# Gate/up products of chunk pairs by seven block products, behind a scaled norm, in a two-layer hybrid network on one core

## The chip, the core and the metric

The kernel runs on one core of a Trainium2 chip. The metric is the device time of one execution in microseconds (us). The engines named below are TensorE (PE, matrix products and transposes, with PEld for its weight loads), VectorE (DVE), ScalarE (ACT), GpSimd (POOL) and SyncE (SP, which issues nearly all DMAs).

## What is computed

The input is one sequence of 256 rows with 1024 features, all in f32. Two layers follow each other. Each has a feed-forward, a mixer and a second feed-forward, each added to the residual stream `h` behind an RMS norm.

```python
def rmsnorm(x, w):
    xf = x.astype(jnp.float32)
    y = xf * lax.rsqrt(jnp.mean(xf * xf, axis=-1, keepdims=True) + EPS)
    return (y * w.astype(jnp.float32)).astype(x.dtype)

def swiglu(x, w_gu, w_down):
    g, u = jnp.split(x @ w_gu, 2, axis=-1)
    return (jax.nn.silu(g) * u) @ w_down
...
    for layer in range(DEPTH):
        h = h + 0.5 * swiglu(rmsnorm(h, ffn1_norm[layer]), ffn1_wgu[layer], ffn1_wd[layer])
        hn = rmsnorm(h, mix_norm[layer])
        ...
        h = h + 0.5 * swiglu(rmsnorm(h, ffn2_norm[layer]), ffn2_wgu[layer], ffn2_wd[layer])
    return rmsnorm(h, final_norm)
```

`w_gu` is 1024 x 5632 (2816 gate columns, then 2816 up columns) and `w_down` 2816 x 1024. The mixer of the first layer is retention and gated linear attention, that of the second a gated linear recurrence and an mLSTM. Both have an input projection of 3600 or 2568 columns, a chain of small work, and an output projection of 1024 x 1024. The change does not touch their arithmetic.

## The kernel before

**Rows and products.** The 256 rows are two halves of 128 (t = 0 and 1). The f32 product is made of three one-pass products: `split` (L101 to L104) writes the high part of a tensor on ACT and the rest, the low part, on DVE, and `mm3` (L181 to L189) adds high x high (L185), high x low weights (L186) and low x high weights (L188). The transposed rows are the stationary operand (128 x 128), the weights the moving one (512 columns at a time).

**Weights.** `load_group` (L109 to L140) brings a group of 128 x 2048 (1 MB) into a `raw` buffer (3 of them) by DMAs of SP and splits it in pieces of 1024 columns (L103, L104; 512 beside the mixers) into `hi` and `lo` buffers (5 of each).

**A feed-forward** (`ffn_units`) has eleven chunks of 256 hidden columns. `a_unit(j)` loads chunk j's 256 gate and 256 up columns, and multiplies each half of the rows: 8 blocks of 128 features x 3 products of 512 columns into one PSUM tile. ACT then makes the silu of the gate (L359), DVE the product with the up half (L361), and PE transposes the result a little later (L201), whose split is `aT`. `b_unit(j)` multiplies `aT` with the chunk's rows of `w_down` into two accumulators `acc` of 512 columns. The units run in the order a0, a1, b0, a2, b1 and so on. The last b unit adds half of `acc` to `h` (`update`) and calls `norm`.

**The norm** (L266 to L288) transposes `h` as it stands (L279), and weights each of the eight blocks as it splits it (`split_w`, L215 and L217). The scale of a row, 1/rms, is computed beside it (`sumsq`) and applied later, where the products are read from PSUM: `scale=rs` on L359, `scalar=rs` on L361, and in the mixers' evacuations. The final norm (L315 to L336) is different: its scale is known before its last multiplication.

**Order.** The second half of the rows follows 1.5 units (LAG) behind the first. Small work is put between the products: `defer(n, fn)` runs `fn` after n more chunks of products or when its result is needed (`flush`). Each engine runs its queue in order, and a tile scheduler writes that order. Constants of a mixer are loaded 14 units ahead of it (`early`).

Of the kernel before, what the change touches and what calls it, by code (L numbers as in the profile page):

```python
# [29 lines left out]
LAG = 1.5  # L30
# delays, in 512-column chunks of the products
# [21 lines left out]
def hybrid_kernel(ctx: ExitStack, tc: tile.TileContext, I, out):  # L53
# [5 lines left out]
    apool = ctx.enter_context(tc.tile_pool(name="act", bufs=1))  # L59
    psum = ctx.enter_context(tc.tile_pool(name="psum", bufs=4, space=bass.MemoryType.PSUM))  # L60
# [40 lines left out]
    def split(src2, hi2, lo2):  # L101
        """src = hi + lo exactly, both carried by one-pass products"""
        S.activation(hi2, src2, AF.Copy)  # L103
        V.tensor_tensor(out=lo2, in0=src2, in1=hi2.bitcast(F32), op=ALU.subtract)  # L104
# [4 lines left out]
    def load_group(src, a, b, fine=False, step=1024, hook=None):  # L109
        """one streamed weight group, seen as [128, a, b] with a * b <= 2048; hook is told of each part to be split"""  # L110
# [70 lines left out]
    def mm3(outs, xT, k, wk, start, stop):  # L181
        """outs: list of (psum, column slice) sharing the stationary chunk k; wk: (hi, lo) views [128, cols]"""
# [13 lines left out]
    def transpose_into(src, n, xT, k0, w=None):  # L196
        """n (<= 4) chunks of 128 columns of src -> xT[:, k0 : k0 + n] in split form, times w by channel"""
# [39 lines left out]
    def norm0(w):  # L237
        """the first norm, among the splits of the first weights"""
# [27 lines left out]
    def norm(t, w, wait=None):  # L266
        """transposed, split, weighted residual; the row scale is left to the evacuations"""
# [3 lines left out]
        def tr():  # L271
            # neighbouring chunks lie in different banks, which the engines then read at one time
# [16 lines left out]

    def get_x(t):  # L290
        flush(lambda: state["xT"][t] is not None)
        return state["xT"][t]
# [5 lines left out]
    # the table set of the feed-forward is there before its first use  # L298
# [7 lines left out]
    def open_pool(name):  # L306
        mixstack.close()
        pools.append(mixstack.enter_context(tc.tile_pool(name=name, bufs=1)))

# [5 lines left out]
    def final_part(t, n):  # L315
        """half of the row: its share of the mean square, and the product with the weights; then the scale"""
# [22 lines left out]
    def ffn_units(wgu, wd, nxt, layer0=False):  # L339
# [4 lines left out]
        def a_unit(j):  # L344
# [4 lines left out]
            def run(t, w):  # L349
                xT = get_x(t)  # L350
                if j == 0:
                    st["acc"][t] = [ps_tile(tag="acc") for _ in range(2)]
                ps = ps_tile()
                for k in range(KC):
# [4 lines left out]
                state["act"] = S.activation(s, ps[:, :FCH], AF.Silu, scale=rs)  # L359
                a = apool.tile([P, FCH], F32, tag="ffa", bufs=2, name=nm("ffa"))  # L360
                state["dve"] = V.scalar_tensor_tensor(out=a, in0=ps[:, FCH:], scalar=rs, in1=s, op0=ALU.mult,  # L361
                                                      op1=ALU.mult)
                aT = [apool.tile([P, 2, P], F32R, tag=f"aT{x}", bufs=4, name=nm("aT")) for x in "hl"]
# [7 lines left out]
        def b_unit(j):  # L371
# [3 lines left out]
            def run(t, w):  # L375
                flush(lambda: (t, j) in st["aT"])
                aT = st["aT"].pop((t, j))
                acc = st["acc"][t]
# [10 lines left out]
                if j == NCHUNK - 1 and nxt is None:  # L389
                    # one half is done while the other is still in the products  # L390
# [8 lines left out]
                if j == NCHUNK - 1:  # L399
                    for n in range(2):  # L400
                        update(n)
                    norm(t, NW[nxt])
            return load, run

        units.append(a_unit(0))
# [769 lines left out]
```

## Time and profile before

| what | before |
|---|---|
| median of 3 runs | 1005.92 us (1005.69 to 1006.1) |
| span of the profiled execution, first to last instruction | 1004.4 us |
| instructions | 12334 |
| DVE: 1024-column and smaller splits of weights and results (L104) | 400, 398.8 us |
| ACT: the same splits' high parts (L103) | 400, 342.7 us |
| PE: products of the three kinds into `ps` | 3 x 928, 357 to 364 us each |
| HBM read, written | 176.15 MB, 1.05 MB |

```profile
DVE  6654545576576654545465455545878765555453
ACT  7544444484455644444454445444998764444442
...
DMA  8956564645247565565656565655334656656521
...
q1 hardware_dynamic: 129736, 177.22, 55.1%
```

These are the page's busy digits: the span is cut in 40 slices, and each digit is the busy share of an engine in tenths. The feed-forwards lie where DVE stands at 4 to 6, the mixers where it rises to 7 and 8. The last line is the queue with nearly all transfers: packets, megabytes, and its share of the sixteen DMA engines' time.

### The profile page before, as it was taken

To read this page: it belongs to the slowest core of one execution; us is meant where nothing else is said; L and a number is where in the kernel's file an instruction comes from. 1 tells how busy PE (TensorE), PEld (TensorE's weight loads), DVE (VectorE), ACT (ScalarE), POOL (GpSimd) and SP (SyncE) were. 2 spreads that over 40 slices of the span, in tenths; PEclk is the share of its full clock that TensorE was granted. 3 is DMA by queue.
4 is the path that set the end of the run, shared out by engine and by line. 5 is a ranking of instruction groups with operands and counts; after the bars stand their busy time and mean duration, and the time that the engine had idled before them with its cause. 6 is when DMAs were issued, how large, how long until landed. Compare 5 with 4: busy or idle time off the path is not lost.

```text
span 1004.4 us, 12334 instructions
## 1 busy us (share of the span) xinstructions
PE 989.5 (99%) x4704; PEld 813.0 (81%) x4704; DVE 585.9 (58%) x945; ACT 529.0 (53%) x877; POOL 22.5 (2%) x54
## 2 busy tenths in 40 slices
PE   7999999999999999999999999999999999999997
PEld 5888888887888888888888888888988888888885
DVE  6654545576576654545465455545878765555453
ACT  7544444484455644444454445444998764444442
POOL 1000000000100000000000000000000000000000
PEclk9999999999999999999999999999999999999999
DMA  8956564645247565565656565655334656656521
GB/s 276 311 177 200 172 206 149 190 132 172 95 168 227 163 210 192 176 202 170 207 168 205 163 205 161 206 167 153 127 126 139 218 168 209 207 166 205 165 96 42
DMA packets 129796, 178.01 MB, mean 177 GB/s; under 512 B 8756, under 2 KB 104900, under 8 KB 129736
## 3 DMA queue, kind: packets, MB, share of 16 engines
q1 hardware_dynamic: 129736, 177.22, 55.1%
q8 instruction: 37, 0.61, 0.2%
q14 instruction: 23, 0.19, 0.1%
HBM read 176.15 MB, written 1.05 MB: 176 GB/s over the span
## 4 chain that ended last, share of the span: by engine, by line
PE 92%; ACT 3%; DMA 2%; DVE 1%; issue 1%; SPq 0%; POOLq 0%; POOL 0%; ACTq 0%
PE ps L185 19%; PE ps L188 19%; PE ps L186 19%; PE acc L185 9%; PE acc L188 9%; PE acc L186 9%; PE ps L201 2%; DMA raw<-in_ffn_wgu_dram 2%; ACT hi L103 1%; DVE lo L104 1%; DMA cum<-in_c_cum_dram 0%; PE acc L615 0%; PE acc L618 0%; PE acc L279 0%; PE acc L481 0%
## 5 line engine op out<-in xcount | busy, mean ns | idle before, releaser
L104 DVE TENSOR_TENSOR lo<-raw,hi 128x1024 fp32r<-128x1024 f32 (+3 forms) x400 | 398.8, 1029 | 262.4 <-ACT hi L103 260.8
L103 ACT ACTIVATE hi<-raw 128x1024 fp32r<-128x1024 f32 (+3 forms) x400 | 342.7, 900 | 244.5 <-PE ps L188 138.1
L185 PE MATMUL ps<-hi,Th 128*128 128x512 f32 (+3 forms) x928 | 364.2, 392 | 1.3 <-ACT Th L215 1.3
L188 PE MATMUL ps<-hi,Tl 128*128 128x512 f32 (+3 forms) x928 | 357.3, 385 | 0.0
L186 PE MATMUL ps<-lo,Th 128*128 128x512 f32 (+3 forms) x928 | 356.6, 384 | 0.0
L185 PEld LDWEIGHTS ps<-hi,Th 128*128 128x128 f32 x928 | 175.3, 189 | 34.7 <-ACT Th L215 1.7
L188 PEld LDWEIGHTS ps<-hi,Tl 128*128 128x128 f32 x928 | 175.0, 189 | 34.6 <-issue 0.2
L186 PEld LDWEIGHTS ps<-lo,Th 128*128 128x128 f32 x928 | 175.5, 189 | 31.8 <-DVE lo L104 0.2
L185 PE MATMUL acc<-hi,aT 128*128 128x512 f32 x352 | 142.7, 405 | 0.0
L186 PE MATMUL acc<-lo,aT 128*128 128x512 f32 x352 | 138.9, 394 | 0.0
L359 ACT ACTIVATE ffs<-ps,rs 128x256 f32<-128x256 f32 x88 | 41.8, 474 | 154.0 <-PE ps L188 154.0
L188 PE MATMUL acc<-hi,aT 128*128 128x512 f32 x352 | 111.0, 395 | 0.0
L361 DVE SCALAR_TENSOR_TENSOR ffa<-ps,rs,ffs 128x256 f32<-128x256 f32 x88 | 42.4, 481 | 92.4 <-ACT ffs L359 92.4
L188 PEld LDWEIGHTS acc<-hi,aT 128*128 128x128 f32 x352 | 66.1, 188 | 15.1
L186 PEld LDWEIGHTS acc<-lo,aT 128*128 128x128 f32 x352 | 66.5, 189 | 13.8
L185 PEld LDWEIGHTS acc<-hi,aT 128*128 128x128 f32 x352 | 66.5, 189 | 13.4
L104 DVE TENSOR_TENSOR aT<-ps,aT 128x256 fp32r<-128x256 f32 x88 | 36.8, 418 | 7.5 <-ACT aT L103 7.5
L103 ACT ACTIVATE aT<-ps 128x256 fp32r<-128x256 f32 x88 | 32.8, 373 | 11.6 <-PE ps L201 11.6
L201 PEld LDWEIGHTS ps<-ident,ffa 128*128 128x128 f32 x176 | 24.6, 140 | 12.3 <-DVE ffa L361 0.6
L201 PE MATMUL ps<-ident,ffa 128*128 128x128 f32 x176 | 33.6, 273 | 0.1
L215 ACT ACTIVATE Th<-ps,nw 128x128 fp32r<-128x128 f32 x56 | 21.0, 375 | 12.9 <-PE ps L279 11.3
L185 PE MATMUL acc<-hi,Th 128*128 128x512 f32 x64 | 25.3, 399 | 0.0
(269 smaller groups left out, 535.9 us busy)
## 6 DMA issues: line engine op xcount, KB each, us to landing
raw<-in_ffn_wgu_dram SPq DMA_DIRECT2D x168, 512.0 KB, 4.9
raw<-in_ffn_wd_dram SPq DMA_DIRECT2D x44, 1024.0 KB, 4.9
raw<-in_e_w_in_dram SPq DMA_DIRECT2D x13, 1024.0 KB, 5.0
raw<-in_o_w_in_dram SPq DMA_DIRECT2D x9, 1024.0 KB, 5.1
raw<-in_e_w_out_dram SPq DMA_DIRECT2D x4, 1024.0 KB, 5.0
raw<-in_o_w_out_dram SPq DMA_DIRECT2D x4, 1024.0 KB, 5.0
raw<-in_ffn_wgu_dram SPq DMA_DIRECT2D x14, 256.0 KB, 6.3
rope<-in_c_rope_dram SPq DMA_DIRECT2D x4, 256.0 KB, 3.9
```

Source lines behind the costliest of these rows:

```text
L103: S.activation(hi2, src2, AF.Copy)
L104: V.tensor_tensor(out=lo2, in0=src2, in1=hi2.bitcast(F32), op=ALU.subtract)
L185: T.matmul(ps, xh[:, k, :], wk[0][:, sl], start=start, stop=False)
L186: T.matmul(ps, xh[:, k, :], wk[1][:, sl], start=False, stop=False)
L188: state["mm"] = T.matmul(ps, xl[:, k, :], wk[0][:, sl], start=False, stop=stop)
L201: T.transpose(pt[:, i * P:(i + 1) * P], src[:, i * P:(i + 1) * P], ident)
L215: last = S.activation(hi, p_, AF.Copy, scale=w[:, k:k + 1])
L359: state["act"] = S.activation(s, ps[:, :FCH], AF.Silu, scale=rs)
L361: state["dve"] = V.scalar_tensor_tensor(out=a, in0=ps[:, FCH:], scalar=rs, in1=s, op0=ALU.mult, op1=ALU.mult)
```

## The change

**Which chunks.** Of the eleven chunks of a feed-forward, six are now made in three pairs; the others are single as before. In the first feed-forward of the network the chunks run 0, 1, then pair 2+3, 4, pair 5+6, 7, pair 8+9, 10; in the other three 0 (its units placed ahead of the rest), pair 1+2, 3, pair 4+5, 6, pair 7+8, 9, 10.

**A pair.** Two chunks together have 512 gate columns G and 512 up columns U. Features are cut in two halves (blocks 0 to 3 and 4 to 7), rows in two halves as well, so that the weights are four 1 MB blocks: r11 (first features, G), r12 (first, U), r21 (second, G), r22 (second, U). The plain way makes eight block products, each of 4 feature blocks x 3 products of 512 columns. The pair makes seven (P1 to P7, Strassen's scheme in Winograd's form): 84 products in place of 96. For that it needs sums of weight blocks, made in place on DVE with 2048 columns an instruction (r12 + r11 for P5; r22 - r12 for P6; r12 - r11 for P7; r21 + r12 for P4), sums of the rows' blocks (S1 to S4, once for each feed-forward), and sums of the results (`cs` tiles). The wide blocks are loaded into `draw` buffers (4), split into the same `hi` and `lo` rings, 2048 columns an instruction, and each result is transposed in four blocks.

**The norm.** Sums over both halves of the rows need rows that are already scaled. `norm_f` therefore computes the row scale first (two sums of squares on ACT, L328 on DVE, the power on POOL), then scales `h` by it and by the norm weights, which a DMA of 512 KB spreads over all partitions (`load_wB`), and transposes the result `hs`. Evacuations of such a feed-forward use no scale. The first feed-forward keeps the old norm for chunks 0 and 1 and gets `norm_f` in addition.

**Order.** A feed-forward is no longer a row of units that the two halves pass 1.5 units apart: its middle part is written out (`main`), with down-projection units (`fill`) between the block products. Down units and output-projection units count half a unit for LAG. The mixer's constants are opened at the feed-forward's last chunk instead of 14 units ahead. There are 8 `aT` buffers instead of 4.

```diff
+PLAN = {
+    True: dict(head=(0, 1), mid=("D2", "a4", "D5", "a7", "D8"), tail=(10,)),
+    False: dict(head=(0,), mid=("D1", "a3", "D4", "a6", "D7", "a9"), tail=(10,)),
+}
+
+TAILB = 3
...
+    def norm_f(t, scaled=False, wait=NT):
...
+        rs = state["rs"][t]
+        if not scaled:
...
+            for n in range(2):
+                sl = slice(n * 512, n * 512 + 512)
+                S.activation(junk[:, sl], h[t][:, sl], AF.Square, scale=D ** -0.5, accum_out=ms[:, n:n + 1])
+            V.scalar_tensor_tensor(out=ms[:, 0:1], in0=ms[:, 0:1], scalar=EPS, in1=ms[:, 1:2], op0=ALU.add, op1=ALU.add)
+            rs = apool.tile([P, 1], F32, tag="rs1", bufs=4, name=nm("rs"))
+            G.tensor_tensor(out=rs, in0=ms[:, 0:1], in1=mh4[:, 0:1], op=ALU.pow)
...
+            for n in range(2):
+                sl = slice(n * 512, n * 512 + 512)
+                V.scalar_tensor_tensor(out=hs[:, sl], in0=h[t][:, sl], scalar=rs, in1=wB[:, sl], op0=ALU.mult,
+                                       op1=ALU.mult)
...
+            for n in range(2):
+                for i in range(4):
+                    T.transpose(pt[n][:, i * P:(i + 1) * P], hs[:, (4 * n + i) * P:(4 * n + i + 1) * P], ident)
+                split(pt[n], f2(xT[0][:, 4 * n:4 * n + 4, :]), f2(xT[1][:, 4 * n:4 * n + 4, :]))
...
+            V.tensor_copy(f[3], pt[0])
+            V.tensor_tensor(out=f[0], in0=pt[1], in1=f[3], op=ALU.subtract)
+            done(1, f[0])
...
+                r = mt("draw", [P, 4, 512], 4)
+                nc.sync.dma_start(r, g[:, k0:k0 + 4, two, :])
...
+                for k in range(4):
+                    for i, (a, b) in enumerate(((0, 0), (0, 1), (1, 0))):
+                        state["mm"] = T.matmul(ps, x[a][:, k, :], w[b][:, k, :], start=first and k == 0 and i == 0,
+                                               stop=k == 3 and i == 2, skip_group_check=not first)
+                    tick(1)
...
+            def p1():
+                d["r11"] = raw(0, 0)
+                y = prod("Y", form(0, 0), parts(d["r11"]), True)
+                d["p1"] = cs()
+                S.activation(d["p1"], y, AF.Copy)
...
+                    add(f2(r), f2(r), f2(d["r11"]))
+                z = prod("Z", sform(1), parts(r), True)
...
+            def p6():
+                d["r22"] = raw(4, 1)
+                add(f2(d["r12"]), f2(d["r22"]), f2(d["r12"]))
+                y = prod("Y", sform(2), parts(d["r12"]), False)
...
+            def p2():
+                d["r21"] = raw(4, 0)
+                x = prod("X", form(0, 1), parts(d["r21"]), True)
+                add(d["p1"], x, d["p1"])
+                S.activation(d["p1"], d["p1"], AF.Silu)
...
+            def p7():
+                add(f2(d["r11"]), f2(d["r12"]), f2(d["r11"]), ALU.subtract)
+                y = prod("Y", sform(3), parts(d["r11"]), False)
+                add(d["p5"], y, d["p5"])
...
+            def p3():
+                z = prod("Z", sform(4), parts(d["r22"]), False)
+                u = d["u1"]
+                add(u, z, u)
+                V.scalar_tensor_tensor(out=u, in0=u, scalar=-1.0, in1=d["p1"], op0=ALU.mult, op1=ALU.mult)
+                out(0, u)
...
+            def p4():
+                add(f2(d["r21"]), f2(d["r21"]), f2(d["r12"]))
+                y = prod("Y", form(1, 1), parts(d["r21"]), False)
...
+                for i in ((5, 6, 7, 3, 4) if n == 0 else (1, 5, 6, 2, 7, 3, 4)):
+                    p[i]()
+                    if i in (5, 2, 3, 4):
+                        fill(1)
```

**Places in the order.** The first place is DVE's queue where the second feed-forward begins, behind the output projection of the first mixer, for the second half of the rows (`h_70`). Before, L453 is the update, L104 the splits of weights and results, and L216 the weighted splits of the transposed rows, eight in a row:

```order
L453 TENSOR_TENSOR h_70<-acc_2665,h_70 128x512
L453 TENSOR_TENSOR h_70<-acc_2666,h_70 128x512
L104 TENSOR_TENSOR lo_2987<-raw_2984,hi_2986 128x1024
L104 TENSOR_TENSOR aT_2840<-ps_2853,aT_2839 128x256
L216 SCALAR_TENSOR_TENSOR Tl_2861<-ps_2887,nw,Th_2860 128x128
L216 SCALAR_TENSOR_TENSOR Tl_2861<-acc_2888,nw,Th_2860 128x128
```

Now, L702 is the update, L115 a split, L336 the scaling, L357 to L360 the sums of the rows' blocks and L531 the sums of weights or results:

```order
L702 TENSOR_TENSOR h_70<-acc_2722,h_70 128x512
L702 TENSOR_TENSOR h_70<-acc_2723,h_70 128x512
L115 TENSOR_TENSOR lo_3014<-draw_3010,hi_3013 128x2048
L328 SCALAR_TENSOR_TENSOR ms_2884<-ms_2884 128x1
L115 TENSOR_TENSOR lo_3040<-raw_3037,hi_3039 128x1024
L336 SCALAR_TENSOR_TENSOR hs_2891<-h_70,rs_2889,wB 128x512 x2
L115 TENSOR_TENSOR lo_3040<-raw_3037,hi_3039 128x1024
L115 TENSOR_TENSOR Tl_2908<-ps_2909,Th_2907 128x512
L115 TENSOR_TENSOR Tl_2908<-acc_2910,Th_2907 128x512
L357 COPY cs_2926<-ps_2909 128x512
L531 TENSOR_TENSOR draw_3010<-draw_3059,draw_3010 128x2048
L358 TENSOR_TENSOR cs_2923<-acc_2910,cs_2926 128x512
```

Between the update and the transposed rows' low parts (`Tl`) there now stand a wide split (P5's weights), a split of down weights and the scaling; and the sums follow, with P6's weight sum among them.

The second place is PE's queue at the same point. Before, two steps of the other half's products (`ps_2880`) stand between the last output products and the transposes of `h_70`:

```order
L188 MATMUL acc_2666<-hi_2717,Tl_2611 128x512
L201 MATMUL ps_2853<-ident,ffa_2837 128x128 x2
L185 MATMUL ps_2880<-hi_2865,Th_2741 128x512
L186 MATMUL ps_2880<-lo_2866,Th_2741 128x512
L188 MATMUL ps_2880<-hi_2865,Tl_2742 128x512
...
L279 MATMUL ps_2887<-ident,h_70 128x128
L279 MATMUL acc_2888<-ident,h_70 128x128
```

Now the twelve products of P1 (`ps_2898`; the first and the last are shown) stand there, then the transposes of the scaled rows `hs_2891`, with P2 (`ps_2964`) behind them:

```order
L199 MATMUL acc_2723<-hi_2738,Tl_2644 128x512
L514 MATMUL ps_2898<-hi_2894,Th_2778 128x512
...
L514 MATMUL ps_2898<-hi_2894,Tl_2779 128x512
L342 MATMUL ps_2909<-ident,hs_2891 128x128 x4
L514 MATMUL ps_2964<-hi_2960,Th_2778 128x512
L342 MATMUL acc_2910<-ident,hs_2891 128x128 x4
L514 MATMUL ps_2964<-lo_2961,Th_2778 128x512
```

The transposes read `hs_2891` in place of `h_70` and moved from behind six products to behind twelve.

The third place is DVE's queue in the middle of the second feed-forward. Before, splits of weights (`raw`) alternate with evacuations:

```order
L104 TENSOR_TENSOR lo_3114<-raw_3111,hi_3113 128x1024 x2
L361 SCALAR_TENSOR_TENSOR ffa_3036<-ps_3009,rs_2919,ffs_3034 128x256
L104 TENSOR_TENSOR lo_3166<-raw_3162,hi_3165 128x1024 x2
L104 TENSOR_TENSOR aT_3039<-ps_3068,aT_3038 128x256
L361 SCALAR_TENSOR_TENSOR ffa_3090<-ps_3058,rs_2781,ffs_3088 128x256
```

Now, at the end of the second pair; `draw_3382` is that pair's r21, `draw_3319` its r12, and `draw_3672` the third pair's r12, whose buffer is that of `draw_3319`; `lo_3486` belongs to P4 of the second pair:

```order
L531 TENSOR_TENSOR cs_3317<-ps_3388,cs_3317 128x512
L115 TENSOR_TENSOR lo_3458<-raw_3455,hi_3457 128x1024 x2
L531 TENSOR_TENSOR draw_3382<-draw_3382,draw_3319 128x2048
L531 TENSOR_TENSOR cs_3339<-ps_3304,cs_3339 128x512
L531 TENSOR_TENSOR draw_3672<-draw_3672,draw_3651 128x2048
L531 TENSOR_TENSOR cs_3380<-ps_3326,cs_3380 128x512
L115 TENSOR_TENSOR lo_3486<-draw_3382,hi_3485 128x2048
L584 SCALAR_TENSOR_TENSOR cs_3380<-cs_3380,cs_3317 128x512
```

The third pair's first sum stands ahead of the split that P4 of the second pair needs.

**Counted in the order of instructions**, over the whole program: products of 512 columns go from 3840 to 3696, transposes and small products of 128 columns from 436 to 452; on DVE instructions of 1024 columns from 256 to 160, of 2048 from 0 to 132, of 512 from 201 to 337, of 256 from 207 to 159, of 128 from 192 to 144; on ACT of 1024 from 268 to 166, of 2048 from 0 to 84, of 512 from 182 to 286, of 128 from 156 to 108.

More of the change, by code (lines that the diff above doesn't have):

```diff
@@ L377, in run @@
                 aT = st["aT"].pop((t, j))
+                if j == 0:
+                    st["acc"][t] = [ps_tile(tag="acc") for _ in range(2)]
                 acc = st["acc"][t]
@@ new lines, in ffn_units, with pre, main @@
+        first = {}
+        def pre():
+            first.update(pair(int(plan["mid"][0][1:])))
+            first[1]()
+            first[2]()
+        def main():
+            for j in plan["head"]:
+                made(j)
+            for n, m in enumerate(plan["mid"]):
+                j = int(m[1:])
+                if m[0] == "a":
+                    step("a", j, 0)
+                    fill(1)
+                    step("a", j, 1)
+                    fill(1)
+                    made(j)
+                    continue
+                p = pair(j) if n else first
+                for i in ((5, 6, 7, 3, 4) if n == 0 else (1, 5, 6, 2, 7, 3, 4)):
+                    p[i]()
+                    if i in (5, 2, 3, 4):
+                        fill(1)
+                made(j)
+                made(j + 1)
+            fill(len(todo))
+            if nxt in FROW:
+                load_wB(nxt)
+            flush(lambda: all((t, i) in st["aT"] for t in range(2) for i in range(NCHUNK - TAILB, plan["tail"][0])))
```

185 lines of the change are left out of this document (159 added, 26 removed).

## The prediction

> **What bounds the kernel now.** I read the page first: the span, the busy shares, the slices and the chain that ended last.
>
> ```profile
> span 1004.4 us, 12334 instructions
> PE 989.5 (99%) x4704; PEld 813.0 (81%) x4704; DVE 585.9 (58%) x945; ACT 529.0 (53%) x877; POOL 22.5 (2%) x54
> ...
> PE   7999999999999999999999999999999999999997
> ...
> PEclk9999999999999999999999999999999999999999
> ...
> PE 92%; ACT 3%; DMA 2%; DVE 1%; issue 1%; SPq 0%; POOLq 0%; POOL 0%; ACTq 0%
> ```
>
> TensorE is busy in every slice but the first and the last, and 92% of the chain lies on it. A busy PE need not be a full one, so I looked at the windows by stage and at who waits for whom, in the middle of a feed-forward.
>
> ```profile
> 100.00:140.00 40.00, 40.00 (x181) 32.83 (x180) 20.34 (x25) 16.86 (x23) 0.00 (x0) 1.00 0.58 182
> ...
> DVE lo L104 <- ACT hi L103: 260.8, 139, 5.9
> ...
> ACT hi L103 <- PE ps L188: 138.1, 48, 4.3
> ```
>
> In 40 us PE works 40.00, VectorE (DVE) 20.34, ScalarE (ACT) 16.86. The waits are those of DVE and ACT; none of PE's reaches the head of that list. So a product taken away is a product won, as long as DVE, which now has half its time free, delivers in time. The timeline gives the price of a product, warm and at the start:
>
> ```profile
> 12.08 0.63 PE L185 MATMUL ps<-hi,Th 128*128 128x512 f32 x1
> 12.51 0.63 PE L186 MATMUL ps<-lo,Th 128*128 128x512 f32 x1
> ...
> 119.98 0.39 PE L188 MATMUL ps<-hi,Tl 128*128 128x512 f32 x1
> ...
> 122.70 0.39 PE L188 MATMUL ps<-hi,Tl 128*128 128x512 f32 x1
> ...
> 336.93 0.27 PE L279 MATMUL acc<-ident,h 128*128 128x128 f32 x1
> ...
> 337.58 0.27 PE L279 MATMUL acc<-ident,h 128*128 128x128 f32 x1
> ```
>
> Between the starts at 119.98 and 122.70 lie twelve products: 0.227 us each (0.39 is the length of one, and they overlap). Six transposes take 0.65: 0.108 each. At the start a product takes 0.43.
>
> **The products.** Counted in the order of instructions, 512-column products go from 3840 to 3696: 12 pairs, each 84 in place of 96. 144 x 0.227 = **32.7 us gone**. Sixteen transposes are added, for the first feed-forward's second normal form: 16 x 0.108 = 1.7.
>
> **What DVE gets.**
>
> ```profile
> 29.63 1.23 DVE L104 TENSOR_TENSOR lo<-raw,hi 128x1024 fp32r<-128x1024 f32 x1 [1.20 <-ACT hi L103]
> 30.77 0.48 DVE L361 SCALAR_TENSOR_TENSOR ffa<-ps,rs,ffs 128x256 f32<-128x256 f32 x1
> 31.17 1.22 DVE L104 TENSOR_TENSOR lo<-raw,hi 128x1024 fp32r<-128x1024 f32 x1
> ...
> 302.11 2.49 DVE L104 TENSOR_TENSOR lo<-raw,hi 128x512 fp32r<-128x512 f32 x4
> ...
> 123.50 2.00 ACT L103 ACTIVATE hi<-raw 128x1024 fp32r<-128x1024 f32 x2
> ```
>
> From start to start a 1024-column instruction costs 1.14, a 256-column one 0.40, a 512-column one 2.49/4 = 0.61. The new 2048-column ones no row shows. Their columns alone cost 2048 x (1.14-0.61)/512 = 2.12, two of 1024 cost 2.28; I take 1.14 + 1.06 = 2.20, and 1.9 for ACT's, just under the 2.00 of two.
>
> A pair loses eight 1024-column splits and four 256-column evacuations (10.7 us) and gets seven wide splits, four wide adds of weights and five 512-column evacuations: 11 x 2.20 + 5 x 0.61 = 27.3. With its own transposed results (four of 256 columns, 1.4) and the two down-projection groups woven in (4.6), DVE needs 33.3 us where PE needs (84 + 48) x 0.227 + 8 x 0.108 = 30.8. A single chunk with its down group takes DVE about 8.3 and PE 16.7. Pair and single together are 41.6 against 47.5: **beside each other they fit**, and what a pair lacks, the single gives back. Hence a second or third pair costs no throughput. What remains are three places where DVE stands in the path.
>
> **Entry of the first feed-forward.** PE does chunk 1's two halves, the sixteen new transposes, P1 and P2 and five products more, 77 x 0.227 plus 22 transposes = 19.9 us, and then needs the low half of P5's weights. Over the same stretch DVE's queue, from the end of chunk 0's second evacuation, holds four wide instructions (8.8), twenty of 512 columns (12.2: scaling, both splits, eleven for the sums S1 to S4 and the first combination) and five of 256 (1.9): 22.9. It starts some 1.4 later (evacuation on ACT and DVE, 0.5 each, and a split that is late) and loses about 0.5 on sums that follow each other directly. Wait: 24.8 - 19.9 = 4.9. Up to P6's weights DVE adds 9.5 (three wide, a down group, S4) to PE's 7.3: 2.2 more. Up to P4's it adds 10.3 to 9.1, with the transposes behind it 1.9 more. **9.0 us.**
>
> **Entry of the other three.** The old norm transposes the row sum as it is and scales later; the new one must know the scale first.
>
> ```profile
> 335.17 1.29 DVE L453 TENSOR_TENSOR h<-acc,h 128x512 f32<-128x512 f32 x2 [1.44 <-PE acc L188]
> ...
> 992.01 0.69 DVE L387 SCALAR_TENSOR_TENSOR h<-acc,h 128x512 f32<-128x512 f32 x1
> ...
> 992.80 0.63 ACT L324 ACTIVATE junk<-h 128x512 bf16<-128x512 f32 x1 [0.68 <-DVE h L387]
> ...
> 993.34 0.18 ACT L324 ACTIVATION_READ_ACCUMULATOR junk<-h 128x1 f32 x1
> ...
> 993.55 0.16 DVE L330 TENSOR_TENSOR ms<-ms 128x1 f32<-128x1 f32 x1
> ...
> 993.85 0.55 POOL L331 TENSOR_TENSOR frs<-ms,mh 128x1 f32<-128x1 f32 x1 [171.53 <-DVE ms L330]
> ...
> 994.43 0.58 DVE L333 TENSOR_SCALAR fo<-hw,frs 128x704 f32<-128x704 f32 x1 [0.72 <-POOL frs L331]
> ```
>
> The old form had the first transpose at 336.82 in the rows above, 1.65 after the update at 335.17 began. The final norm is the new chain: from the update's end (992.70) to the scaled product 1.73. For the first half of the rows that chain ends at about 4.0 after the last output product, when 4.1 us of the other half's products are behind PE: covered. For the second half only P1 covers it (12 products, 2.7). Here DVE has the update (1.3), then P5's split (2.2), the sum, half a down split and the scaling (0.6 a half): the first scaled half is there 5.8 to 6.2 after the last product, less the 2.7 of P1: **3.2 us** of wait. In the second layer's last feed-forward a wide add stands in place of the half split, one more. Afterwards PE meets DVE again at P4: the add of its weights, two evacuations that wait for P7 and P3, the product and the split follow each other, 2.1 us of wait. With small ones 5.8, 5.8 and 6.9: **18.5 us.**
>
> **The reload of the third pair.** In the last three feed-forwards the third pair's first weight sum stands on DVE two rows behind P4's sum of the second pair, ahead of P4's split. It needs a load into a buffer which that very sum is the last to read.
>
> ```profile
> raw<-in_ffn_wd_dram SPq DMA_DIRECT2D x44, 1024.0 KB, 4.9
> ```
>
> A megabyte lands 4.9 after its issue; one 512-column row (0.6) stands between. So behind P4's sum come 5.1 of loading, 2.2 for the sum, 0.6, and 2.2 for P4's split: 10.1. Counted from P2's end the sum is done at 5.3, the split at 15.4, and PE, with two down units, P7, P3 and seven products (12.6), waits 2.8, and a little at the next transposes: **3.0 each, 9.0.** Its floor is a landing like the quickest of the smaller loads, near 3: one us each.
>
> **The sum.** -32.7 + 1.7 + 9.0 + 18.5 + 9.0 = +5.5 on the span: 1009.9. The runs' median of 1005.92 lies 1.5 above the span: **1011 us**. The constants of the mixers are loaded later than before, but 27 us of PE's work ahead of their use; I cost them at nothing, and about 5 (their landing) if that cover were gone.
>
> **A rule on the clock.** The first products step by 0.43 and later ones by 0.227, and the granted clock of before never fell inside the span; no wait of PE there is long enough to show whether it would. The Trainium skill, page "TensorE: Matmul & The Clock Gate", section "What's actually happening", says that the array falls back to half its clock after an idle window of about 3.4 us and needs as long of work to come back. By it, waits like the 4.9, 3.2 and 4.2 above would bring the slow step back, and the sum would be some 6 us higher.
>
> **The rivals.**
> *Faster: DVE's queue is shorter than I count.* Each wait is the difference of two sums of 20 to 40 us. With 2.12 a wide instruction, no loss on dependent ones and a landing of 3, the first entry falls to 5, the others to 10 together, the reload to 3: 18, and the time is 1005.9 - 32.7 + 1.7 + 18 = 993. It decides once the waits are under 29. For it: DVE has slack over each feed-forward as a whole. Against it: its queue is in order, and PE's rows behind a waiting one are too. Chance 0.26. If all waits are hidden, 975: 0.07.
> *Slower: the clock falls.* Each of four entries with a wait over 3 us brings back seven products at 0.43 in place of 0.227, 1.4 each: 1017. For it, the slow start; against it, no row with a fall. 0.12.
> *Slower: the later pairs wait too,* because a wide split needs ACT's 1.9 before DVE's 2.2 and a sum before both: 1.2 in each of eight pairs, 1021. 0.08.
> *No difference,* the waits between 29 and 33: 0.11. That fewer products are issued than written is excluded by the count.
>
> **How the numbers follow.** Forecast 1008 to 1016: 0.36. Faster by over 0.2% (what a measurement of this kernel can tell, 2 us): 0.33; within: 0.11; slower: 0.36 + 0.12 + 0.08 = 0.56. The range from 985 to 1020 takes in the shorter queue and the clock, and leaves out the fully hidden case and the worst.
>
> **What would show it.** The slices of PE must show eights where the four feed-forwards begin. The waits must list PE behind DVE's low halves of the wide weights, behind the scaled row sum, and DVE behind a load of the wide weights three times, about 4 us each. DVE's wide instructions must stand at 2.1 to 2.3, and its busy sum near 780. I am wrong if PE's idle time is under 30 us in all (15 of them there before), if the third pair's load is early, or if the steps of PE rise above 0.23 behind the waits.

## The result, and the profile after

The changed kernel takes **1022.5 us** (median of 4 runs, 1021.2 to 1022.75), the kernel before in the same comparison 1005.81 (4 runs). The ratio is 1.0166 (95% interval 1.0151 to 1.018): slower by 16.7 us. The forecast was 1011 with a range up to 1020. Its sign was right, its size was not.

The page of the changed kernel, with the lines that answer to those of before:

```profile
span 1021.0 us, 12081 instructions
...
PE 979.0 (96%) x4576; PEld 795.6 (78%) x4576; DVE 812.9 (80%) x1027; ACT 605.7 (59%) x872; POOL 24.7 (2%) x48
...
PE   7799999999999899999998999999999979999997
...
DVE  6989989477576888999559999965789889999843
...
PEclk9989999999999899999999999999999999999999
...
PE 81%; DVE 8%; issue 4%; ACT 3%; DMA 2%; POOL 1%; SPq 0%; POOLq 0%; ACTq 0%; DVEq 0%
```

Read the two digit rows one above the other. PE has an 8 or a 7 in slices 2, 14, 22 and 33, where the four feed-forwards begin. PEclk, the clock that TensorE was granted, shows an 8 in slices 3 and 14; before it had none. PE fell from 92% of the chain to 81%. PE's idle time rose from 14.9 to 42.0 us, and yet its busy time fell by only 10.5 us, although 144 products (33 us) are gone. So there are two losses: PE waits, and while it works it works more slowly.

PE's own waits in the changed kernel (total, times, longest):

```profile
PE ps L342 <- DVE hs L336: 13.4, 6, 4.1
PE ps L514 <- DVE lo L115: 9.7, 5, 4.9
...
PE ps L540 <- DVE cs L584: 1.3, 2, 0.6
```

And windows of 40 us at the four beginnings and, last, in the middle of a feed-forward (length, then PE, PEld, DVE, ACT and POOL busy, granted clock, DMA share, GB/s):

```profile
40.00:80.00 40.00, 32.73 (x123) 24.73 (x122) 35.76 (x34) 22.36 (x26) 0.00 (x0) 0.87 0.49 166
340.00:380.00 40.00, 35.26 (x149) 28.03 (x148) 33.44 (x37) 20.22 (x26) 1.47 (x1) 0.91 0.30 105
540.00:580.00 40.00, 34.36 (x151) 27.77 (x152) 37.26 (x39) 23.43 (x29) 1.46 (x1) 0.96 0.46 153
820.00:860.00 40.00, 34.83 (x152) 27.66 (x152) 36.05 (x37) 23.22 (x29) 2.54 (x1) 0.96 0.40 138
880.00:920.00 40.00, 40.00 (x179) 32.55 (x178) 37.84 (x29) 25.69 (x27) 0.00 (x0) 1.00 0.55 186
```

In the middle PE works 40.00 of 40 with 179 instructions (181 in such a window before), though DVE is at 37.84. At the beginnings it executes 123 to 152. The granted clock there is 0.87 to 0.96. The first beginning in single rows shows how the two losses hang together:

```profile
44.30 0.47 PE L196 MATMUL acc<-hi,aT 128*128 128x512 f32 x1 [0.24 <-DVE cs L362]
49.66 0.79 PE L514 MATMUL ps<-lo,S1h 128*128 128x512 f32 x1 [4.88 <-DVE lo L115]
50.25 0.63 PE L514 MATMUL ps<-hi,S1l 128*128 128x512 f32 x1
50.67 0.63 PE L514 MATMUL ps<-hi,S1h 128*128 128x512 f32 x1
...
55.76 0.39 PE L196 MATMUL acc<-hi,aT 128*128 128x512 f32 x1
55.99 0.39 PE L197 MATMUL acc<-lo,aT 128*128 128x512 f32 x1
```

PE waits 4.88 for the low half of P5's weights, then takes 0.42 from product to product until about 55, and 0.23 again afterwards. In the records of the granted clock the half clock lasts 6.8 us here. Inside the span there are six stretches of half clock that the kernel before does not have, two of 6.8 us and four of 3.4, 27.3 us together.

### The profile page after: what moved, and what is told of

It is laid out like the page before. It is cut to its first block, busy times and chain, and to the rows that moved or that the text cites. A ratio compares the mean times of both kernels' runs of the same rounds, so it can differ in the third digit from the quotient of the medians.

```text
span 1021.0 us, 12081 instructions
## 1 busy us (share of the span) xinstructions
PE 979.0 (96%) x4576; PEld 795.6 (78%) x4576; DVE 812.9 (80%) x1027; ACT 605.7 (59%) x872; POOL 24.7 (2%) x48
## 4 chain that ended last, share of the span: by engine, by line
PE 81%; DVE 8%; issue 4%; ACT 3%; DMA 2%; POOL 1%; SPq 0%; POOLq 0%; ACTq 0%; DVEq 0%
PE ps L514 20%; PE ps L196 11%; PE ps L199 11%; PE ps L197 11%; PE acc L197 7%; PE acc L199 7%; PE acc L196 7%; DVE lo L115 4%; ACT hi L114 1%; DMA draw<-in_ffn_wgu_dram 1%; PE ps L540 1%; PE ps L212 1%; POOL rs L330 1%; DMA h<-in_x_dram 1%; DVE cs L531 0%
## 5 line engine op out<-in xcount | busy, mean ns | idle before, releaser
L115 DVE TENSOR_TENSOR lo<-raw,hi 128x1024 fp32r<-128x1024 f32 (+2 forms) x304 | 282.9, 967 | 49.6 <-ACT hi L114 49.1
L114 ACT ACTIVATE hi<-raw 128x1024 fp32r<-128x1024 f32 (+2 forms) x304 | 241.2, 850 | 61.5 <-PE ps L199 32.9
L196 PE MATMUL ps<-hi,Th 128*128 128x512 f32 (+3 forms) x544 | 213.5, 393 | 1.5 <-ACT Th L226 1.4
L197 PE MATMUL ps<-lo,Th 128*128 128x512 f32 (+3 forms) x544 | 207.6, 382 | 0.0
L199 PE MATMUL ps<-hi,Tl 128*128 128x512 f32 (+3 forms) x544 | 207.3, 381 | 0.0
L115 DVE TENSOR_TENSOR lo<-draw,hi 128x2048 fp32r<-128x2048 f32 x84 | 190.6, 2285 | 19.6 <-ACT hi L114 19.6
L114 ACT ACTIVATE hi<-draw 128x2048 fp32r<-128x2048 f32 x84 | 160.0, 1919 | 64.7 <-DVE draw L531 44.1
L196 PEld LDWEIGHTS ps<-hi,Th 128*128 128x128 f32 x544 | 103.3, 190 | 21.4 <-ACT Th L226 1.8
L197 PEld LDWEIGHTS ps<-lo,Th 128*128 128x128 f32 x544 | 103.5, 190 | 17.6 <-DVE lo L115 0.4
L531 DVE TENSOR_TENSOR draw<-draw,draw 128x2048 f32<-128x2048 f32 x48 | 109.7, 2285 | 2.3 <-DMA draw<-in_ffn_wgu_dram 2.0
L115 DVE TENSOR_TENSOR aT<-ps,aT 128x256 fp32r<-128x256 f32 x88 | 37.0, 420 | 28.6 <-ACT aT L114 28.4
```

The costliest lines, as they stand in the source:

```text
L196: T.matmul(ps, xh[:, k, :], wk[0][:, sl], start=start, stop=False)
L197: T.matmul(ps, xh[:, k, :], wk[1][:, sl], start=False, stop=False)
L199: state["mm"] = T.matmul(ps, xl[:, k, :], wk[0][:, sl], start=False, stop=stop)
L531: state["dve"] = V.tensor_tensor(out=out, in0=a, in1=b, op=op)
```

## What the experiments were to tell apart

**Theory A**: the loss lies where the feed-forwards begin; PE waits there for the scaled rows and for P5's and P4's weights, and each wait is made longer by the half clock behind it. **Theory B**: DVE (80% busy) has too much to do throughout the pairs; the half clock only stands beside that. The prediction also had a charge of 9 us for the third pairs' reload, which needed a test of its own. Below, "excess" is the time from one PE start to the next, less the median of that width (0.231 for 512 columns, 0.109 for 128), summed over a stretch. In the changed kernel it is 12.9 us at the first beginning, 11.5, 8.7 and 8.9 at the others, and 0.1 to 0.8 in the rest of each feed-forward. The runs below were measured in several sessions; the kernel before took 1005.0 to 1006.0 in each of them, so times of different sessions compare to about 1 us.

**1 and 2: useless products in the wait.**

```diff
+            if not layer0:
+                x0 = get_x(0)[0]
+                px = fd["X"] = ps_tile()
+                for i in range(WARM):
+                    with after(state["mm"]):
+                        state["warm"] = T.matmul(px, x0[:, i % 8, :], f2(x0[:, 0:4, :]), start=i == 0, stop=i == WARM - 1)
+                tick(2)
```

This piece stands between P1 and P2. Both runs also hold the transposes of the scaled rows behind these products, and the scaling is written apart from the transposes.

> The transposes of the second half of the scaled rows are held behind P1 and one added product whose result nobody reads, in the last three feed-forwards; DVE's order moves so that in two of them a wide weight sum (2.28 us) stands ahead of the scaling in place of a split of 1.22. Control for the next run. Theory A (the time lies in waits where a feed-forward begins, and each is made longer by the half clock that follows it): about 1 us more in each of two, 1022.5 + 2 = 1024 to 1026. Theory B (the pairs cost DVE too much everywhere, the half clock only stands beside it): the same, 1022 to 1025.

Measured: 1018.48 us (1017.72 to 1019.07). Both theories had it at 1022 or more, and the control is 4.0 us quicker than the changed kernel. In the profiles 2.6 of 3.7 us lie in the first feed-forward, which has the same two waits at P4 (0.18 and 1.45) and no fall of the clock behind them. The next run is compared with this one, not with the changed kernel.

> As the run before, with sixteen such products (3.6 us of PE) in place of one, ahead of the transposes that PE waits for. They do no work that is needed. Theory A: three stretches of half clock (6.8, 3.4 and 3.4 us in the changed kernel's records) vanish, and with them 1.7 to 3 us each: 5 to 8 us less than with one product, 1017 to 1020. Theory B: no more than 1 us either way, 1023 to 1026.

Measured: 1012.91 us (1010.44 to 1013.28), **5.6 us less for 45 more products**. Windows of 4 us behind the wait of the second feed-forward, with one product and then with sixteen:

```profile
351.00:355.00 4.00, 4.00 (x13) 3.14 (x12) 4.00 (x5) 0.41 (x1) 0.00 (x0) 0.62 0.70 252
```

```profile
351.00:355.00 4.00, 4.00 (x20) 3.29 (x19) 4.00 (x6) 2.29 (x2) 0.00 (x0) 1.00 0.41 87
```

PE is "busy" 4.00 in both and does 13 instructions in one and 20 in the other; the clock is 0.62 and 1.00. With sixteen, the profiled execution has no half clock left in the last three feed-forwards. With one, the records show 17.1 us of it there (and 3.4 in the second mixer, which the kernel before has too and run 2 has not). The scaled rows were as late as before; only the clock was saved. This supports A and shows that a wait of 4 to 5 us costs nearly 2 more behind it.

**3: no weight sums.**

```diff
-                    add(f2(r), f2(r), f2(d["r11"]))
...
-                add(f2(d["r12"]), f2(d["r22"]), f2(d["r12"]))
...
-                add(f2(d["r11"]), f2(d["r12"]), f2(d["r11"]), ALU.subtract)
...
-                add(f2(d["r21"]), f2(d["r21"]), f2(d["r12"]))
```

> Leaves out the 48 wide sums of weight blocks (2.28 us each, 110 us of DVE in all); the loads, the splits and all products stay, so the output is not the reference's. Theory A: the wait of 4.9 at the first feed-forward shrinks by one sum (2.3) and perhaps loses its half clock (3), the waits at P4 (0.8 + 3.8 + 4.1 + 2.5 + 1.1 us with their half clock) go, the waits for the scaled rows stay: 12 to 17 us less, 1005 to 1011. Theory B: DVE is then no longer short anywhere, 25 us or more less, under 998.

Measured: 998.36 us (996.21 to 998.55), between the two and next to B's bound of 998. What went is what stood at the beginnings, since the changed kernel has only 0.1 to 0.8 elsewhere in a feed-forward. The excess of the first beginning is gone entirely, and that at P4 too; the waits for the scaled rows remain (11.5 us, longest 4.1). A had mis-sized the first beginning: I took one sum and its clock off it, but with the sums gone no part of its 12.9 was left.

**4: two pairs in place of three** in the last three feed-forwards.

```diff
-    False: dict(head=(0,), mid=("D1", "a3", "D4", "a6", "D7", "a9"), tail=(10,)),
+    False: dict(head=(0,), mid=("D1", "a3", "D4", "a6", "a7", "a8", "a9"), tail=(10,)),
```

> In the last three feed-forwards the third pair is made as two single chunks: 36 products more, no other change of plan. Theory A: a late pair costs almost nothing beside its products, so its loss is 3 x (12 x 0.232 - 0.5) = 7 us: 1028 to 1031. The step of the prediction on the reload (3.0 us for each third pair): 3 x (2.8 - 3.0), 1021 to 1023. Theory B: the pairs cost more than they bring, so the time falls, under 1020.

Measured: 1031.53 us (1027.0 to 1031.94), 9.0 more. A third pair is worth 3.0 us (to about 1, since the runs spread over 4.9 us); its twelve products alone are 12 x 0.229 = 2.75. So a late pair costs little or nothing beside its products, which speaks against B and against the prediction's reload. The trace of the changed kernel shows why. DVE first, then SP's queue, in the second feed-forward:

```profile
411.70 6.70 DVE L115 TENSOR_TENSOR lo<-draw,hi 128x2048 fp32r<-128x2048 f32 x3 [0.23 <-ACT hi L114]
...
421.19 2.28 DVE L531 TENSOR_TENSOR draw<-draw,draw 128x2048 f32<-128x2048 f32 x1
...
425.34 2.29 DVE L531 TENSOR_TENSOR draw<-draw,draw 128x2048 f32<-128x2048 f32 x1 [1.26 <-DMA draw<-in_ffn_wgu_dram]
```

```profile
416.23 2.57 SPq L499 DMA_DIRECT2D draw<-in_ffn_wgu_dram  x2
...
423.50 7.33 SPq L499 DMA_DIRECT2D draw<-in_ffn_wgu_dram  x2
```

SP's two loads in the first row are the third pair's r11 and r12. The second was issued at 416.23 + 2.57 - 0.37 (the length of one issue) = 418.4, just when the third of the three splits above ended, which is P3's, of r22. P4's sum of r21 and r12 began only at 421.19. So the third pair's r12 went into r22's buffer, not into r12's as the text on the third place in the order says, and its load was under way 5 us earlier than I had it. DVE waited 1.26 for it, and the excess on PE there is 0.8.

**5, 6 and 7: where the feed-forward begins.** The fifth run has two single chunks ahead of the first pair in the last three feed-forwards and the transposes behind 36 of their products; the sixth also has three single chunks ahead in the first; the seventh takes pairs and scaled norm out of the first alone.

```diff
-    False: dict(head=(0,), mid=("D1", "a3", "D4", "a6", "D7", "a9"), tail=(10,)),
+    False: dict(head=(0, 1), mid=("D2", "a4", "D5", "a7", "D8"), tail=(10,)),
...
-            norm_f(t)
+            norm_f(t, wait=12 if t else NT)
```

The sixth has this in addition, and the seventh, from the changed kernel, the piece below it:

```diff
-    True: dict(head=(0, 1), mid=("D2", "a4", "D5", "a7", "D8"), tail=(10,)),
+    True: dict(head=(0, 1, 2), mid=("D3", "a5", "D6", "D8"), tail=(10,)),
```

```diff
+        if layer0:
+            units.append(a_unit(0))
+            for j in range(1, NCHUNK):
...
+                units.append(a_unit(j))
+                units.append(b_unit(j - 1)[:2])
```

> In the last three feed-forwards two single chunks stand ahead of the first pair (0 and 1, then pairs 2+3, 5+6, 8+9) in place of one, and the transposes of the second half's scaled rows come behind 36 of their products in place of 12. As many products, sums and pairs as in the changed kernel. Theory A (waits where a feed-forward begins, each made longer by half clock): the excess at the three begins (6.8 + 5.8 + 6.0 us) goes, and most of that at P4 (4.1 + 2.5 + 1.1), since DVE has a chunk more time: 18 to 26 less, 997 to 1004. Theory B (DVE short everywhere in the pairs; the run without weight sums was 24 us quicker): only what useless products brought too, 1012 to 1017.

Measured: 1010.92 us (1009.31 to 1012.86), 11.6 less in place of 18 to 26: short of A, and 1 us under B's range. The waits for the scaled rows are gone (0.4 at most), but PE now waits in P2:

```profile
352.68 0.50 PE L514 MATMUL ps<-hi,Th 128*128 128x512 f32 x1 [1.13 <-ACT hi L114]
355.00 0.50 PE L514 MATMUL ps<-lo,Th 128*128 128x512 f32 x1 [1.11 <-DVE lo L115]
```

The five split buffers were full with the two leading chunks and P1, so P2's split could start only when P1 was done (run 9, which moves P2, has no such wait). At P4 1.85 to 2.2 remained. A new wait took the place of the old one, but a shorter one, without half clock in the last three feed-forwards.

> As the run before, and in the first feed-forward three single chunks ahead of the first pair (0, 1, 2, then pairs 3+4, 6+7, 8+9, with 5 and 10 single), still three pairs. Theory A: the first begin's excess (8.4 + 0.8 + 3.8) goes as well, 10 to 13 us less than the run before: 985 to 993. Two pairs stand side by side, where the prediction's sums have DVE at 33.3 us against PE's 30.8: at most 3 us back. Theory B: no more than 3 us less than the run before.

Measured: 1011.61 us (1008.41 to 1012.56): no gain, as B said. The first feed-forward is 1.1 shorter than in run 5, with 8.3 us of excess between 53 and 82 and 2.8 later on, beside the two neighbouring pairs; the next two are 1.5 longer each, with 3.4 us of half clock again.

> The first feed-forward alone as it was before the change: no pairs, no second norm, units in the old order; the other three as in the changed kernel. Theory A: 36 products more (+8.3 us), 16 transposes fewer (-1.7) and the excess of the first begin gone (-13.0): 1014 to 1018. If pairs cost elsewhere in the first feed-forward too: under 1012. If the first begin's excess is only moved: 1022 or more.

Measured: 1015.23 us (1013.14 to 1017.83), as A had it. In the first feed-forward the pairs and their norm cost 7 us more than they save.

**8: P4's weights early.**

```diff
+                add(f2(d["r21"]), f2(d["r21"]), f2(d["r12"]))
+                d["w4"] = parts(d["r21"])
+                lo4 = state["lo"]
+                z = prod("Z", sform(4), w3, False)
...
+                with after(lo4):
+                    add(d["p5"], d["y7"], d["p5"])
+                    add(u, z, u)
```

> The changed kernel with one move in every pair: P4's weight sum and its split stand on DVE ahead of the two sums that read the results of P7 and P3 (before, P4's split stood behind them and so behind P3's last product). No work added or taken away. Theory A (PE waits at P4 because of this order): the excess at P4 (3.8 + 4.1 + 2.5 + 1.1, with its half clock) goes, and 0.5 in other pairs: 8 to 12 less than 1022.5, 1010 to 1015. Theory B (DVE has too much to do in the pairs whatever its order): the wait comes back elsewhere, 1019 to 1024.

Measured: 1024.9 us (1023.06 to 1027.09): a miss for A, and 0.9 over B's range. DVE's rows show it, and the one of PE behind them:

```profile
371.71 2.29 DVE L531 TENSOR_TENSOR draw<-draw,draw 128x2048 f32<-128x2048 f32 x1
375.99 2.29 DVE L115 TENSOR_TENSOR lo<-draw,hi 128x2048 fp32r<-128x2048 f32 x1 [1.99 <-ACT hi L114]
378.19 1.28 DVE L531 TENSOR_TENSOR cs<-ps,cs 128x512 f32<-128x512 f32 x2
```

```profile
379.03 0.47 PE L514 MATMUL ps<-hi,Th 128*128 128x512 f32 x1 [2.31 <-DVE cs L531]
```

P4's split directly behind its sum leaves DVE idle for 1.99 while ACT makes the high part, and P7's result, whose accumulator P4 goes on with, is read after that. PE waits 2.31 for it instead. The wait at P4 is not a matter of that order alone. With a chunk more time ahead (run 9, below) the same order leaves an excess of 1.3 to 1.5 there, in place of 6.4, 6.3 and 1.9 in the last three feed-forwards here.

**9, 10 and 11: both together.** Two leading chunks, P4's weights early, P2 moved behind the leading chunks' second halves, and the transposes behind 27 products; the tenth with the first feed-forward as before the change (as in run 7); the eleventh with three leading chunks in it (as in run 6).

```diff
             first[1]()
-            first[2]()
+            if layer0:
+                first[2]()
...
+            if not layer0:
+                first[2]()
             for n, m in enumerate(plan["mid"]):
```

> Two leading single chunks as in the run with the second single, with P4's weights early, and P2 behind the second half's leading chunks (it waited there for a free split buffer: 1.13 + 1.11), the transposes of the scaled rows after 27 products. Theory A: the three remaining waits of each of those feed-forwards (3.1 + 0.8 + 2.2) go, and P4's in the first: 1010.9 - 18 - 3 = 988 to 994. Theory B: 1003 or more.

Measured: 999.4 us (997.64 to 1000.95), ratio to the kernel before 0.994 (0.9924 to 0.9957). It lies between A's range and B's. The waits in P2 are gone, but the gain over run 5 is a little over half of what I wrote: the three still have an excess of about 3 to 5 us each, the last one with a wait of 1.94 for a down-projection's operand.

> The run before, with the first feed-forward as before the change (no pairs in it). Theory A: what that was worth in the changed kernel (7.3) less P4's part of it (3): 984 to 991. It would be the first that beats the kernel before by over 1%.

Measured: **996.65 us** (994.43 to 999.05), ratio 0.9912 (0.9889 to 0.9934), quicker than both kernels, if by less than expected (A had 984 to 991). Its page:

```profile
span 995.7 us, 12099 instructions
...
PE 972.6 (98%) x4596; PEld 793.0 (80%) x4596; DVE 750.8 (75%) x996; ACT 584.1 (59%) x864; POOL 20.6 (2%) x48
...
PEclk9999999999999999999999999999999999999999
```

> As the run without a plain first feed-forward, with three single chunks ahead of its first pair and P2 behind them. Theory A: the first feed-forward's excess is gone but for its pairs side by side: 980 to 989. If DVE is short over the whole first feed-forward: 990 or more.

Measured: 1001.91 us (10 runs, 1000.1 to 1007.01). A miss: the first feed-forward became 3.6 longer than in run 9, with 4.7 us of excess at 64 to 72 and 6.1 at 140 to 149. In the first feed-forward, with its second norm and its pairs side by side, B fits better than A; I did not take it apart further.

**12: the power alone.** DVE's split or weight sum between the sum of squares and the scaling is put behind the scaling.

```diff
-                add(f2(d["r12"]), f2(d["r22"]), f2(d["r12"]))
+                with after(state["hsi"]):
+                    add(f2(d["r12"]), f2(d["r22"]), f2(d["r12"]))
```

> The changed kernel with DVE's order changed at one point of the last three feed-forwards: the scaling of the second half's rows stands directly behind the sum of squares, ahead of the split (1.22) or weight sum (2.28) that stood between them, so that DVE runs nothing beside POOL's power. Theory C (POOL's power of 128x1 takes 0.55 alone and 1.47, 1.46 and 2.54 beside a DVE instruction of two SBUF inputs, because it gets through only when that one ends): the power takes 0.55 in all three, PE's waits for the scaled rows fall from 4.1 to about 3.1, 3.1 and 2.1, 4 us together, and 2 to 6 more where a stretch of half clock goes: 1012 to 1018. If the power's length has another reason: 1.5 and 2.5 again, 1021 to 1024.

Measured: 1023.63 us (1022.81 to 1024.84). The power took 0.55 to 0.56 in all three, as theory C had it, but the time did not fall: in the second and the fourth feed-forward the order moved a weight sum ahead of the update of `h`, and PE waited 4.64. In the third, where the update kept its place, the wait fell from 4.10 to 3.26, near theory C's 3.1, and a new wait of 1.94 at 559 took the gain away:

```profile
536.99 0.55 POOL L330 TENSOR_TENSOR rs<-ms,mh 128x1 f32<-128x1 f32 x1 [17.32 <-DVE ms L328]
538.47 1.09 PE L342 MATMUL ps<-ident,hs 128*128 128x128 f32 x4 [3.26 <-DVE hs L336]
```

The stages of five kernels, each from the last product of the stage before it (start times) to its own last product, in us:

| stage | before | changed | lead (5) | lead, P2 late (9) | and plain first (10) |
|---|---|---|---|---|---|
| feed-forward 1 | 203.1 | 214.0 | 212.9 | 211.7 | 203.5 |
| mixer 1 | 131.9 | 129.0 | 129.0 | 129.0 | 132.8 |
| feed-forward 2 | 188.2 | 193.4 | 187.7 | 184.3 | 184.3 |
| feed-forward 3 | 185.7 | 190.4 | 187.5 | 184.0 | 184.0 |
| mixer 2 | 106.5 | 104.3 | 102.6 | 103.9 | 103.9 |
| feed-forward 4 | 181.9 | 182.9 | 180.9 | 179.4 | 179.6 |

## Why the prediction was right and wrong

**The step that failed: the slow clock, put at nothing in the sum.** The prediction summed 9.0 + 18.5 = 27.5 us at the four beginnings, all of it waiting. PE did stand idle there for 26.4, but the excess is 42.0. Most of the difference lies in products behind the waits that step by 0.43 in place of 0.23: in the six stretches of half clock the longer steps add up to about 12 us (summed from the trace). The prediction named this as a rival, with 6 us and a chance of 0.12, "against it, no row with a fall". That reading was wrong. The page's digits cover 25 us each, and a 9 stands for anything from 90%; in single rows the kernel before has a fall inside the span, at 754.6 in the second mixer:

```profile
753.65 1.22 PE L925 MATMUL acc<-wi,sel 4*128 4x128 f32 x8
754.80 0.80 PE L188 MATMUL ps<-hi,Tl 128*128 128x512 f32 x1
755.40 0.63 PE L185 MATMUL ps<-hi,Th 128*128 128x512 f32 x1
755.82 0.63 PE L186 MATMUL ps<-lo,Th 128*128 128x512 f32 x1
```

Products step by 0.43 there, for 3.4 us. The time was still nearer than its terms were, because the reload was charged 9.0 and cost 1.2. Two of the prediction's own signs of being wrong came true: the third pair's load was early, and the steps behind the waits rose above 0.23.

**What bounds the kernel: right.** PE sets the end, and a product is worth its step: 144 x 0.229 = 33.0 us were saved, and in the middle of a feed-forward pairs cost PE nothing (40.00 of 40 above; 3.0 us for each third pair in run 4).

**Wide instructions: right.** Three in a row took DVE 6.70 above, and one 2.28, so the step is 4.42 / 2 = 2.21, against 2.20; ACT's took 1.92, against 1.9. DVE's busy sum came to 812.9, against 780.

**First beginning: the first wait right, its price not.** 4.9 was forecast at P5 and 4.88 came; at P6 0.5 in place of 2.2; at P4 1.45 + 0.18 in place of 1.9. That is 7 us of waiting in place of 9.0, but an excess of 12.9. The 4.9 came out partly by luck: PE took 20.9 up to that product in place of 19.9, and DVE's low half was done 0.9 later than summed, and the two cancelled.

**The other three: the waits near.** For the scaled rows 3.2 was forecast twice and 4.2 in the last feed-forward; 4.1 came each time. At P4 it was 2.1, where 0.65 + 1.31 came twice and 0.73 in the last. The chain in the changed kernel's second feed-forward:

```profile
343.55 1.28 DVE L702 TENSOR_TENSOR h<-acc,h 128x512 f32<-128x512 f32 x2
...
345.44 2.29 DVE L115 TENSOR_TENSOR lo<-draw,hi 128x2048 fp32r<-128x2048 f32 x1 [0.62 <-ACT hi L114]
...
347.72 1.22 DVE L115 TENSOR_TENSOR lo<-raw,hi 128x1024 fp32r<-128x1024 f32 x1
347.88 1.47 POOL L330 TENSOR_TENSOR rs<-ms,mh 128x1 f32<-128x1 f32 x1 [16.47 <-DVE ms L328]
349.39 1.42 DVE L336 SCALAR_TENSOR_TENSOR hs<-h,rs,wB 128x512 f32<-128x512 f32 x2 [0.45 <-POOL rs L330]
350.29 1.09 PE L342 MATMUL ps<-ident,hs 128*128 128x128 f32 x4 [4.09 <-DVE hs L336]
```

The power took 1.47, where I had put the final norm's 0.55. That is the missing 0.9; the third feed-forward of run 12, with 0.55, waited 3.26. The first half of the rows, costed as covered, also gave an excess of 0.7 to 1.0 in each. Together the three have 29.1, in place of 18.5.

**The clock: the rival that came true.** It took six falls, two of them with 6.8 us at half clock. Runs 1 and 2 give a second price. Their profiled executions, with spans of 1017.3 and 1008.7, differ by 8.6 us and by 20.5 us of half clock (the mixer's stretch with it); at that rate the 27.3 us that the changed kernel has more cost 11.5 (an estimate from those two executions). The medians of the two runs lie only 5.6 apart: the profiled execution of run 2 is its quickest, and the granted clock of its other three was 0.993, not 0.995. The Trainium skill, page "TensorE: Matmul & The Clock Gate", section "What's actually happening", gives a free-running window of 3413 ns and half clock after an idle one; the stretches of 3.4 and 6.8 us agree with that window. Two of the falls, at 72.3 and 382.9 in the trace, came behind these waits only:

```profile
69.10 1.20 PE L196 MATMUL acc<-hi,aT 128*128 128x512 f32 x4 [0.18 <-ACT hi L114]
71.75 0.50 PE L514 MATMUL ps<-lo,Th 128*128 128x512 f32 x1 [1.45 <-DVE lo L115]
...
379.91 0.66 PE L540 MATMUL ps<-ident,cs 128*128 128x128 f32 x4 [0.65 <-DVE cs L584]
...
382.11 0.50 PE L514 MATMUL ps<-lo,Th 128*128 128x512 f32 x1 [1.31 <-DVE lo L115]
```

So here a window that was about half idle was enough. It was not always: the same 0.65 + 1.31 in the third feed-forward, and the same 0.18 + 1.45 in run 1, had no fall behind them. And the fall at 754.6 above came without any wait, behind two runs of eight products of only four rows (1.13 and 1.22 us). What exactly sets the limit, the runs do not show.

**The reload: wrong.** 9.0 us were charged and an excess of about 1.2 came in all. The step that failed here is "it needs a load into a buffer which that very sum is the last to read": the buffer was another one, free 5 us earlier.

**Not foreseen:** the mean step of products that follow each other (those under 0.3) rose from 0.2289 to 0.2303, 5 us over 3600 products. It did so as well in run 3, without the sums; I did not find the cause.

The sum with what was measured: -33.0 + 1.7 + 42.0 (the beginnings) + 1.2 + 5.0 = +16.9, against +16.6 between the two spans. The table of stages gives the same total, with the two mixers 2.9 and 2.2 shorter; whether they are quicker or only their borders moved I did not split.

## What to carry to other kernels

Where PE is the bound, a scheme that trades products for sums pays in the steady part, as long as the busiest other engine keeps up over a pair and its neighbour; its price is paid at the start of each stage, where the sums' inputs do not exist yet. So give the start work that needs no sum: one more plain chunk ahead of the first pair in three of the feed-forwards brought the change from 1.7% slower to 0.7% slower, P2 behind those chunks and P4's weights early to 0.6% quicker, and leaving the first stage out to 0.9%. Price each wait of 4 us on PE with the slow products behind it (behind waits of 1 to 2.5 us some places had a fall and others none), look for slow steps in single rows and not in the page's digits, and read which buffer a load goes into from the order of the loads, not from the names' order.

## What was not expected of the hardware

A power of 128 x 1 on POOL took 0.55 to 0.56 wherever DVE was idle. Beside DVE instructions with two SBUF inputs it took 1.47, 1.46 and 2.54, and ended 0.4 after the DVE instruction each time. DVE and POOL in the changed kernel's last feed-forward, and POOL in run 12:

```profile
836.12 2.29 DVE L531 TENSOR_TENSOR draw<-draw,draw 128x2048 f32<-128x2048 f32 x1
...
836.29 2.54 POOL L330 TENSOR_TENSOR rs<-ms,mh 128x1 f32<-128x1 f32 x1 [17.16 <-DVE ms L328]
```

```profile
348.24 0.56 POOL L330 TENSOR_TENSOR rs<-ms,mh 128x1 f32<-128x1 f32 x1 [18.54 <-DVE ms L328]
```

The Trainium skill, page "SBUF — State Buffer", section "SBUF: two separate sides", says that such a DVE instruction and a GpSimd one that reads SBUF lock the shared port pair against each other for a whole instruction. Run 12, which took the DVE instruction away, agrees: 0.55 to 0.56. No run put a DVE instruction of another kind beside the power. And useless products can make a kernel quicker: 45 of them, 10 us of PE at full clock, saved 5.6 us.
